# Attention of a streaming-encoder layer: 128-query pieces, paired banks, fewer copies at a block's end

## The chip, the cores and the metric

The kernel runs on one core of a Trainium2 chip. Its time is device microseconds (us) of one execution. The kernel before takes 4123.1 us, the median of three runs (4122.56 to 4125.78). A profiled execution, from which all durations below come, took 4126.18 us, with a span of 4124.6 us between its first and last instruction.

The engines are PE (TensorE, matmuls), DVE (VectorE, elementwise work), ACT (ScalarE, activations and copies), POOL (GpSimd) and SP (SyncE, which issues DMA transfers). PE writes its results to PSUM, a memory of eight banks, each of which holds 512 fp32 numbers per partition; ACT and DVE read them from there.

## The reference, cut to what matters

One layer of a trunk: a joint input projection, a recurrent group (RG-LRU), a group of eight attention heads, an output projection, a mixture of experts and a per-layer embedding, over 4096 tokens of width 1024. The change touches the attention alone. Its reference, for blocks of 128 queries and 8 heads of width 64:

```python
for qb in range(S // Q_BLOCK):
    lo, hi = qb * Q_BLOCK, (qb + 1) * Q_BLOCK
    s = jnp.einsum('bhqd,bhkd->bhqk', q[:, :, lo:hi], k[:, :, :hi]) * scale
    s = s + cum_logf[:, :, lo:hi, None] - cum_logf[:, :, None, :hi]
    mask = jnp.arange(hi)[None, :] <= jnp.arange(lo, hi)[:, None]
    pr = jax.nn.softmax(jnp.where(mask, s, -jnp.inf), axis=-1)
    outs.append(jnp.einsum('bhqk,bhkd->bhqd', pr, v[:, :, :hi]))
```

`cum_logf` is a running sum of the logarithms of forget gates, so a key's weight falls with its distance from the query.

## The kernel before, in words

The program runs in stages: projection and recurrence (to about 1060 us of the profiled execution), attention (to about 1790 us), output projection and router, then the experts and the embedding. Attention works in 64 units: a unit is a head `h` and a block `b` of 512 queries. Scores are laid out with 128 keys on the partitions and queries along the row, so one matmul takes a tile of 128 keys and up to 512 queries.

For each head, ranked by how fast its gates forget, two tables set what is computed. `NEAR` is the reach of the keys that enter the softmax, `WIN` the reach of those that are only looked at. For each unit `pieces` (L542) makes two lists of banks: `near` and `far`. A bank is a list of pieces (key tile, first query, last query, place in the bank). In the kernel before a piece is 256, 384 or 512 queries wide; a piece that reaches fewer queries is widened to 256, and two of 256 share a bank. The four key tiles on the diagonal are pieces of 512, 384, 256 and 256 queries; the triangle is masked by a small bf16 matmul (`mask`, L606).

Each unit passes four steps:

- The max pass (`max_pass`, L649): one matmul for each piece into a bank of the pool `psM` (tile `psm`), then a running maximum `mx` over the banks: ACT copies the first bank (L667), DVE folds in one piece after the other (L669). POOL reduces `mx` over the partitions (L672) and writes the result into the row of queries `Q2` and `Q3`, by which later matmuls subtract it.
- The scores (`scores`, L690): near banks are taken two at a time, as a group. For each piece two matmuls (L703, L704) fill a bank `pss` of the pool `psS`, and ACT takes two exponentials of each bank, one rounded for the matmul (`ph`, L708) and one full (`pf`, L709).
- The correction (`low`, L714): DVE computes `pl`, which is `pf` less `ph`, in one instruction over both banks where they are equally long (L720), and otherwise in one for each (L723).
- The values (`pv`, L725): for each piece one fp32 matmul of `ph` (L743) and four narrow bf16 matmuls (L751 to L753), two groups after the group's scores. They accumulate in `O`, two banks that neighbouring units use in turn: `acc` is the unit's own, `alt` the other one's row 96, where a part of value row 0 is kept. At a block's end ACT makes three copies out of `O` (L763 to L765), DVE one sum (L766), and POOL issues two DMA transfers (L768, L769).

The far banks are only looked at (`look`, L678): one matmul for each piece into a bank `psf` of the pool `psM`, and one exponential with a running sum (L688), whose result decides whether a head's far keys can be left out.

The pools `psM` and `psS` have three banks each, `O` has two: all eight. The order of PE's instructions is written out by the loop at the end of the stage: scores of the group's first bank, a step of the max pass (and a look) from `between`, the second bank, another step, remaining looks, and the values of the group two before. The max pass runs 14 banks ahead (`LEAD`). The other engines' order is set by a scheduler.

Of the kernel before, what the change touches and what calls it, by code (L numbers as in the profile page):

```python
# [10 lines left out]
F32 = mybir.dt.float32  # L11
# [32 lines left out]
NFB = 8  # L44
# [15 lines left out]
def hybrid_block(ctx: ExitStack, tc: tile.TileContext, I, out, T, caps, dbg=None, upto=9):  # L60
# [456 lines left out]
    with tc.tile_pool(name="dk0", bufs=1) as dk0, tc.tile_pool(name="dq", bufs=1) as dqp, \  # L517
            tc.tile_pool(name="dp", bufs=2) as dp, tc.tile_pool(name="dk1", bufs=1) as dk1, \
            tc.tile_pool(name="dob", bufs=2) as dob, \
            tc.tile_pool(name="psM", bufs=3, space=PSUM) as psM, tc.tile_pool(name="psS", bufs=3, space=PSUM) as psS, \  # L520
# [11 lines left out]
        maskb = dqp.tile([P, 2 * P], BF16, name="maskb")  # L532
        V.tensor_copy(identb, ident)
        V.memset(maskb, 0.0)
        V.memset(maskb[:, 0:P], NEG)
        G.affine_select(maskb[:, P:2 * P], maskb[:, P:2 * P], pattern=[[1, P]], compare_op=ALU.is_ge, fill=NEG,
# [4 lines left out]

        def pieces(u):  # L542


            r, b = units[u]
            nn, nw = NEAR[r] // P, WIN[r] // P
            near = [[(4 * b, 0, 512, 0)], [(4 * b + 1, P, 512, 0)]]
            half = [(4 * b + 2, 256, 512), (4 * b + 3, 256, 512)]
            rest = []
            for j in range(1, min(4 * b, nw) + 1):  # L550
                kt = 4 * b - j
                w = 0 if j > nn else max(256, min(512, (nn - j + 1) * P))
                f = min(512, (nw - j + 1) * P)
                if w > 256:
                    near.append([(kt, 0, w, 0)])
                elif w:
                    half.append((kt, 0, w))
                if f > w:
                    rest.append((kt, w, min(512, max(f, w + 256))))
            near += [[(*p, 256 * i) for i, p in enumerate(half[k:k + 2])] for k in range(0, len(half), 2)]  # L560
            far = []
            for kt, c0, c1 in sorted(rest, key=lambda p: p[1] - p[2]):
                for bank in far:
                    at = bank[-1][3] + bank[-1][2] - bank[-1][1]
                    if at + c1 - c0 <= 512:
                        bank.append((kt, c0, c1, at))
                        break
                else:
                    far.append([(kt, c0, c1, 0)])
            return near, far  # L570
# [35 lines left out]
        def mask(ps, b, kt, c0, at):  # L606
            d = kt - 4 * b
            if d == 3:
                PE.matmul(ps[:, at:at + 256], identb, maskb, start=False, stop=True)
            elif d >= 0:  # L610
                o = at + d * P - c0
                PE.matmul(ps[:, o:o + P], identb, maskb[:, P:2 * P], start=False, stop=True)  # L612
# [65 lines left out]
        def look(u, k):  # L678
# [3 lines left out]
            bank = plan[u][1][k]  # L682
            ps = psM.tile([P, 512], F32, tag="m", name="psf")
            for kt, c0, c1, at in bank:
                PE.matmul(ps[:, at:at + c1 - c0], K2[i][0:KR, kt * P:(kt + 1) * P], Q3[qi][0:KR, c0:c1], start=True, stop=True)
            n = length(bank)
            jf = dp.tile([P, 512], BF16, tag="jf", bufs=2, name="jf")
            S.activation(jf[:, 0:n], ps[:, 0:n], AF.Exp, bias=fbias, accum_out=gm[:, u, k:k + 1])  # L688

        def scores(u, banks, between):  # L690
# [5 lines left out]
            pf = dp.tile([P, 2, 512], F32, tag="pf", bufs=2, name="pf")  # L696
            for a, bank in enumerate(banks):
                ps = psS.tile([P, 512], F32, tag="s", name="pss")
                for kt, c0, c1, at in bank:
# [3 lines left out]
                    PE.matmul(ps[:, at:e], K1[i][:, ks], q1[:, c0:c1], start=True, stop=False)  # L703
                    PE.matmul(ps[:, at:e], K2[i][0:KR, ks], Q2[qi][0:KR, c0:c1], start=False, stop=not dg)  # L704
                    if dg:
                        mask(ps, b, kt, c0, at)
                n = length(bank)
# [1191 lines left out]
```

## Time and profile before

| | us |
|---|---|
| median of three runs | 4123.1 |
| profiled execution | 4126.18 |
| its span | 4124.6 |
| attention, 1080 to 1780 us: length | 700.0 |
| of it ACT busy | 634.0 |
| of it PE busy | 629.4 |
| of it DVE busy | 519.8 |
| of it POOL busy | 334.9 |

An instruction's duration runs from its start until its result is written; the next one may start before that. The distance from one start to the next is called a step below. PE's durations are modelled and overlap one another, so its busy time is not a measure of how much work it could take.

### The profile page before, as it was taken

The numbers are of one execution on the slowest core, as the hardware profiler recorded it, in microseconds if no ns is written. First come the engines' busy times: TensorE is split into PE (matmuls) and PEld (weight loads), VectorE is DVE, ScalarE is ACT, GpSimd is POOL, SyncE is SP. The second block draws the span as 40 slices with busy tenths as digits, with TensorE's granted clock in tenths as the row PEclk, the third lists the DMA queues.
The fourth block names the chain that finished last, engine by engine and source line by source line (L and its number), as shares of the span: only waits on it lengthen the run. The fifth ranks groups of instructions, "written<-read, shape, count | busy, mean of one in ns | idle before, by whom it ended". The sixth has DMA issues, their size and how long they took to land. (4 is left out here: it accounts for less than half of the span.)

```text
span 4124.6 us, 63126 instructions
## 1 busy us (share of the span) xinstructions
PE 3908.7 (95%) x21955; PEld 3191.5 (77%) x21955; DVE 2662.6 (65%) x5513; ACT 2240.8 (54%) x3823; POOL 598.1 (15%) x719
## 2 busy tenths in 40 slices
PE   8999998999788889979999699999999999999999
PEld 7878876777455556657788488899998999988887
DVE  5445456777777777778887345566665566566666
ACT  4333235777688999953333335556565555552222
POOL 0000000000343445601111111101111111100000
PEclk9999998999899999989999899999999999999999
DMA  6445343221443445554443546666776666664454
GB/s 221 132 128 162 124 133 103 67 67 49 113 122 104 118 120 137 146 149 133 138 122 98 187 142 201 209 229 234 239 234 208 215 228 227 224 233 159 158 181 146
DMA packets 331451, 653.59 MB, mean 158 GB/s; under 512 B 40170, under 2 KB 163306, under 8 KB 331123
## 3 DMA queue, kind: packets, MB, share of 16 engines
q1 hardware_dynamic: 263729, 516.96, 40.0%
q0 software_dynamic: 30880, 81.75, 6.0%
q10 hardware_dynamic: 36514, 50.74, 3.9%
q8 instruction: 177, 2.90, 0.3%
q14 instruction: 151, 1.24, 0.1%
HBM read 507.24 MB, written 147.31 MB: 159 GB/s over the span
## 5 line engine op out<-in xcount | busy, mean ns | idle before, releaser
L105 DVE TENSOR_TENSOR ul<-raw,uh 128x1024 fp32r<-128x1024 f32 x410 | 497.1, 1222 | 155.2 <-ACT uh L104 154.7
L111 PE MATMUL psg<-xh,uh 128*128 128x256 f32 (+5 forms) x1600 | 510.9, 319 | 0.8 <-ACT xh L107 0.8
L112 PE MATMUL psg<-xl,uh 128*128 128x256 f32 (+5 forms) x1600 | 504.9, 316 | 0.0
L113 PE MATMUL psg<-xh,ul 128*128 128x256 f32 (+5 forms) x1600 | 504.7, 315 | 0.0
L104 ACT CAST uh<-raw 128x1024 fp32r<-128x1024 f32 x410 | 424.0, 1046 | 58.6 <-DMA raw<-in_w_exp_dram 58.2
L111 PEld LDWEIGHTS psg<-xh,uh 128*128 128x128 f32 x1600 | 303.7, 190 | 13.8 <-ACT xh L107 1.2
L112 PEld LDWEIGHTS psg<-xl,uh 128*128 128x128 f32 x1600 | 303.9, 190 | 9.4 <-DVE xl L108 0.5
L113 PEld LDWEIGHTS psg<-xh,ul 128*128 128x128 f32 x1600 | 303.7, 190 | 8.7
L669 DVE TENSOR_TENSOR mx<-psm,mx 128x256 f32<-128x256 f32 (+2 forms) x438 | 220.1, 510 | 95.2 <-PE psm L662 56.3
L708 ACT ACTIVATE ph<-pss 128x512 fp32r<-128x512 f32 (+1 forms) x386 | 224.3, 581 | 57.7 <-PE pss L612 20.8
L111 PE MATMUL psy<-uh,hid 128*128 128x512 f32 (+2 forms) x608 | 250.2, 412 | 0.0
L113 PE MATMUL psy<-uh,hid 128*128 128x512 f32 (+2 forms) x608 | 240.1, 395 | 0.0
L112 PE MATMUL psy<-ul,hid 128*128 128x512 f32 (+2 forms) x608 | 240.1, 395 | 0.0
L170 PE MATMUL z<-wh,xh 128*128 128x512 f32 x768 | 227.3, 400 | 8.7 <-ACT wh L107 8.7
L170 PE MATMUL z<-wl,xh 128*128 128x512 f32 x768 | 224.4, 397 | 2.0 <-DVE wl L108 2.0
L709 ACT ACTIVATE pf<-pss 128x512 f32<-128x512 f32 (+1 forms) x386 | 225.4, 584 | 0.0
L170 PE MATMUL z<-wh,xl 128*128 128x512 f32 x768 | 222.4, 395 | 0.0
L111 PE MATMUL pso<-wo,yh 128*128 128x512 f32 x512 | 206.8, 404 | 5.9 <-ACT yh L104 5.9
L112 PE MATMUL z<-xl,wh 128*128 128x512 f32 x512 | 202.1, 396 | 9.3 <-DVE xl L105 9.3
L224 ACT ACTIVATE sq<-z,rcol 128x512 f32<-128x512 f32 x64 | 43.6, 686 | 306.3 <-PE z L170 306.2
L112 PE MATMUL pso<-wo,yh 128*128 128x512 f32 x512 | 204.5, 399 | 5.3 <-issue 5.3
L111 PE MATMUL pg<-uh,xh 128*128 128x512 f32 x512 | 205.8, 402 | 1.2 <-ACT xh L104 1.2
(468 smaller groups left out, 10197.3 us busy)
## 6 DMA issues: line engine op xcount, KB each, us to landing
raw<-in_w_exp_dram SPq DMA_DIRECT2D x408, 512.0 KB
xraw<-in_xT_dram ACTq DMA_DIRECT2D x128, 256.0 KB
raw<-d_y SPq DMA_DIRECT2D x64, 512.0 KB
d_v<-vt SPq DMA_DIRECT2D x32, 520.0 KB
VT<-d_v SPq DMA_DIRECT2D x64, 260.0 KB
d_x<-x SPq DMA_DIRECT2D x16, 1028.0 KB
xr<-in_x_dram SPq DMA_DIRECT2D x32, 512.0 KB
K<-d_kh SPq DMA_DIRECT2D x128, 128.0 KB
```

The lines of the kernel that those rows point to most:

```text
L104: S.copy(hi, src)
L105: V.tensor_sub(lo, src, fv(hi))
L111: PE.matmul(ps, sh, mh, start=first, stop=False)
L112: PE.matmul(ps, sh, ml, start=False, stop=False)
L113: PE.matmul(ps, sl, mh, start=False, stop=last)
L170: PE.matmul(zs[j], x[k // 2][:, xs], w[k % 2][:, j * 512:(j + 1) * 512], start=(kc == 0 and k == 0), stop=(kc == KC - 1 and k == 2))
L224: S.activation(sq[:, j, :], zs[j], AF.Square, scale=r)
L669: V.tensor_tensor(mx[:, c0:c1], ps[:, at:at + c1 - c0], mx[:, c0:c1], op=ALU.max)
L708: S.activation(ph[:, a, 0:n], ps[:, 0:n], AF.Exp)
L709: S.activation(pf[:, a, 0:n], ps[:, 0:n], AF.Exp)
```

## The change

Pieces become exactly as wide as their reach, in multiples of 128 queries, and `packed` puts them into banks, longest first, as many as fit; full banks come first. The diagonal's fourth piece is 128 wide and its mask, like the others, 128 columns. Counted by the two versions of `pieces` over the 64 units: the near lists have 502 pieces as before; 116 of the 234 that were 256 queries wide are now 128; their columns go from 182,656 to 167,808, their banks from 386 to 339 (318 full ones), their groups from 205 to 191 (137 of two full banks, 33 of one full bank, 21 others). The far lists have 329 pieces, 93,824 columns and 190 banks before and after.

The pool `psS` now has two buffers of two banks, and `psM` two banks. A group's scores fill one buffer of `psS`, and then one exponential `ph` and one `pf` go over both banks. `look` takes two far banks at once, fills a buffer of `psS` instead of one of `psM`, and takes one exponential over both: 108 in place of 190. Looks no longer stand in `between`, but all behind the group's scores. `low` always works bank by bank. At a block's end ACT keeps one copy; DVE copies row 96 of the other bank to a row `rw` (one buffer) and adds to it; POOL issues three DMA transfers in place of two.

```diff
-NFB = 8
+NFB = 4
...
-            tc.tile_pool(name="psM", bufs=3, space=PSUM) as psM, tc.tile_pool(name="psS", bufs=3, space=PSUM) as psS, \
+            tc.tile_pool(name="psM", bufs=2, space=PSUM) as psM, tc.tile_pool(name="psS", bufs=2, space=PSUM) as psS, \
...
+        def packed(pieces):
+
+            banks = []
+            for kt, c0, c1 in sorted(pieces, key=lambda p: p[1] - p[2]):
+                for bank in banks:
+                    if length(bank) + c1 - c0 <= 512:
+                        bank.append((kt, c0, c1, length(bank)))
+                        break
+                else:
+                    banks.append([(kt, c0, c1, 0)])
+            return sorted(banks, key=lambda b: -length(b))
...
-            near = [[(4 * b, 0, 512, 0)], [(4 * b + 1, P, 512, 0)]]
-            half = [(4 * b + 2, 256, 512), (4 * b + 3, 256, 512)]
-            rest = []
+            near = [(4 * b + d, d * P, 512) for d in range(4)]
+            far = []
             for j in range(1, min(4 * b, nw) + 1):
-                kt = 4 * b - j
-                w = 0 if j > nn else max(256, min(512, (nn - j + 1) * P))
+                w = max(0, min(512, (nn - j + 1) * P))
                 f = min(512, (nw - j + 1) * P)
...
+                if w:
+                    near.append((4 * b - j, 0, w))
                 if f > w:
-                    rest.append((kt, w, min(512, max(f, w + 256))))
...
+                    far.append((4 * b - j, w, f))
+            return packed(near), packed(far)
...
-            if d == 3:
-                PE.matmul(ps[:, at:at + 256], identb, maskb, start=False, stop=True)
-            elif d >= 0:
+            if d >= 0:
                 o = at + d * P - c0
-                PE.matmul(ps[:, o:o + P], identb, maskb[:, P:2 * P], start=False, stop=True)
+                PE.matmul(ps[:, o:o + P], identb, maskb, start=False, stop=True)
...
-            bank = plan[u][1][k]
-            ps = psM.tile([P, 512], F32, tag="m", name="psf")
-            for kt, c0, c1, at in bank:
-                PE.matmul(ps[:, at:at + c1 - c0], K2[i][0:KR, kt * P:(kt + 1) * P], Q3[qi][0:KR, c0:c1], start=True, stop=True)
-            n = length(bank)
-            jf = dp.tile([P, 512], BF16, tag="jf", bufs=2, name="jf")
-            S.activation(jf[:, 0:n], ps[:, 0:n], AF.Exp, bias=fbias, accum_out=gm[:, u, k:k + 1])
+            ps = psS.tile([P, 2, 512], F32, tag="s", name="psf")
+            banks = plan[u][1][2 * k:2 * k + 2]
+            for a, bank in enumerate(banks):
+                for kt, c0, c1, at in bank:
+                    PE.matmul(ps[:, a, at:at + c1 - c0], K2[i][0:KR, kt * P:(kt + 1) * P], Q3[qi][0:KR, c0:c1], start=True, stop=True)
+            jf = dp.tile([P, 1024], BF16, tag="jf", bufs=1, name="jf")
+
+            n = 512 * (len(banks) - 1) + length(banks[-1])
+            assert len(banks) == 1 or length(banks[0]) == 512
+            S.activation(jf[:, 0:n], ps.rearrange("p a n -> p (a n)")[:, 0:n], AF.Exp, bias=fbias, accum_out=gm[:, u, k:k + 1])
...
+            ps = psS.tile([P, 2, 512], F32, tag="s", name="pss")
             for a, bank in enumerate(banks):
-                ps = psS.tile([P, 512], F32, tag="s", name="pss")
...
-                n = length(bank)
-                S.activation(ph[:, a, 0:n], ps[:, 0:n], AF.Exp)
-                S.activation(pf[:, a, 0:n], ps[:, 0:n], AF.Exp)
                 if a == 0:
                     between()
+            n = 512 * (len(banks) - 1) + length(banks[-1])
+            assert len(banks) == 1 or length(banks[0]) == 512
+            for t in (ph, pf):
+                S.activation(t.rearrange("p a n -> p (a n)")[:, 0:n], ps.rearrange("p a n -> p (a n)")[:, 0:n], AF.Exp)
             return u, banks, ph, pl, pf
...
-            ns = [length(bank) for bank in banks]
-            if len(ns) == 2 and ns[0] == ns[1]:
-                if a == 0:
-                    n = ns[0]
-                    V.tensor_tensor(pl[:, :, 0:n], pf[:, :, 0:n], fv(ph)[:, :, 0:n], op=ALU.subtract)
-            elif a < len(ns):
-                n = ns[a]
+            if a < len(banks):
+                n = length(banks[a])
                 V.tensor_tensor(pl[:, a, 0:n], pf[:, a, 0:n], fv(ph)[:, a, 0:n], op=ALU.subtract)
...
+                rw = dob.tile([1, 512], F32, tag="rw", bufs=1, name="rw")
                 sm = dob.tile([64, 512], F32, tag="sm", name="sm")
-                ob = dob.tile([65, 512], F32, tag="ob", name="ob")
+                ob = dob.tile([64, 512], F32, tag="ob", name="ob")
+
                 S.copy(sm, acc[64:128])
-                S.copy(sm[0:1], alt[96:97])
-                S.copy(ob[64:65], acc[64:65])
-                V.tensor_tensor(ob[0:64], acc[0:64], sm, op=ALU.add)
+                V.tensor_copy(rw, alt[96:97])
+                V.tensor_tensor(ob, acc[0:64], sm, op=ALU.add)
+                V.tensor_tensor(rw, acc[0:1], rw, op=ALU.add)
                 et = ACE if u == len(units) - 1 else PLE_
-                E.dma_start(d_o[bass.ds(head(h, 2, et), HD), bs], ob[0:64])
-                E.dma_start(d_den[bass.ds(head(h, 0, et), 1), bs], ob[64:65])
+                E.dma_start(d_o[bass.ds(head(h, 2, et), 1), bs], rw)
+                E.dma_start(d_o[bass.ds(head(h, 2, et) + 1, HD - 1), bs], ob[1:HD])
+                E.dma_start(d_den[bass.ds(head(h, 0, et), 1), bs], sm[0:1])
...
-                mine = list(range(len(far)))
+                nf = (len(far) + 1) // 2
+                mine = list(range(nf))
                 if ng > 1:
-                    mine = mine[len(far) * max(0, g - 1) // (ng - 1):len(far) * g // (ng - 1)]
+                    mine = mine[nf * max(0, g - 1) // (ng - 1):nf * g // (ng - 1)]
...
-                    if mine:
-                        look(u, mine.pop(0))
                     if prev:
```

How this moves instructions on ACT, around the end of a block of the third head. The two buffers of `O` carry numbers, the other tiles are named as above; sizes are partitions by columns. Before:

```order
L688 ACTIVATE jf,gm<-psf,fbias 128x512
L708 ACTIVATE ph<-pss 128x512
L709 ACTIVATE pf<-pss 128x512
L763 COPY sm<-O_8693 64x512
L765 COPY ob<-O_8693 1x512
L764 COPY sm<-O_8694 1x512
L708 ACTIVATE ph<-pss 128x384
L709 ACTIVATE pf<-pss 128x384
```

And after, around the end of a block of the same head:

```order
L709 ACTIVATE ph<-pss 128x1024
L709 ACTIVATE pf<-pss 128x1024
L685 ACTIVATE jf,gm<-psf,fbias 128x1024
L758 COPY sm<-O_8692 64x512
L709 ACTIVATE ph<-pss 128x1024
L709 ACTIVATE pf<-pss 128x1024
```

Two of the three copies are gone from ACT, and each exponential covers both banks of a group.

On DVE, the instructions around a block's end before:

```order
L669 TENSOR_TENSOR mx<-psm,mx 128x512
L720 TENSOR_TENSOR pl<-pf,ph 128x1024
L669 TENSOR_TENSOR mx<-psm,mx 128x512
L766 TENSOR_TENSOR ob<-O_8693,sm 64x512
L723 TENSOR_TENSOR pl<-pf,ph 128x384
```

And after:

```order
L663 TENSOR_TENSOR mx<-psm,mx 128x384
L663 TENSOR_TENSOR mx<-psm,mx 128x128
L759 COPY rw<-O_8693 1x512
L716 TENSOR_TENSOR pl<-pf,ph 128x512 x2
L760 TENSOR_TENSOR ob<-O_8692,sm 64x512
L761 TENSOR_TENSOR rw<-O_8692,rw 1x512
L663 TENSOR_TENSOR mx<-psm,mx 128x384
```

Two instructions on one row of `O` have come to DVE at each block's end, with corrections and maxima of other groups queued between and behind them.

On PE, one group with a look after the change, from its scores to the values of the group two before:

```order
L700 MATMUL pss<-q_13895,K_8677 128x384
L701 MATMUL pss<-Q_8698,K_8679 128x384
L700 MATMUL pss<-q_13895,K_8677 128x128
L701 MATMUL pss<-Q_8698,K_8679 128x128
L656 MATMUL psm<-Q_8700,K_8679 128x384
L656 MATMUL psm<-Q_8700,K_8679 128x128
L700 MATMUL pss<-q_13895,K_8677 128x256
L701 MATMUL pss<-Q_8698,K_8679 128x256
...
L680 MATMUL psf<-Q_8704,K_8679 128x256 x2
L680 MATMUL psf<-Q_8704,K_8679 128x384
L736 MATMUL O_8692<-ph,VT_8681 128x512 x2
```

The step of the max pass stands between the two banks of a pair that now get their exponentials together, and the look fills the other buffer of the same pool.

## Rows read from the trace of the kernel before

**Rows 1.** Busy time by stretch: us, PE, PEld, DVE, ACT, POOL, PE clock, DMA share, GB/s.

```profile
1080.00:1780.00 700.00, 629.43 (x4808) 406.94 (x4806) 519.78 (x879) 634.02 (x1408) 334.88 (x434) 0.98 0.46 123
1558.00:1708.00 150.00, 144.17 (x1167) 94.91 (x1163) 119.64 (x195) 144.35 (x322) 84.53 (x107) 1.00 0.53 143
```

**Rows 2.** Waits from 1058 to 1782 us: us in total, times, longest.

```profile
PE O L743 <- ACT sm L764: 30.5, 33, 2.6
PE psf L685 <- ACT mx L667: 17.8, 11, 1.9
```

**Rows 3.** ACT's groups, 1080 to 1780 us: count, busy us, mean ns, idle before.

```profile
L688 ACT ACTIVATE jf<-psf,fbias 128x512 bf16<-128x512 f32 x179 | 127.1, 714 | 0.1
L764 ACT COPY sm<-O 1x512 f32<-1x512 f32 x62 | 35.9, 580 | 1.5
L765 ACT COPY ob<-O 1x512 f32<-1x512 f32 x62 | 35.8, 577 | 1.5
```

**Rows 4.** Timeline, ACT and PE, at a block's end: start, us, instruction.

```profile
1501.58 0.58 ACT L765 COPY ob<-O 1x512 f32<-1x512 f32 x1
1502.18 0.58 ACT L764 COPY sm<-O 1x512 f32<-1x512 f32 x1
1502.78 0.49 ACT L708 ACTIVATE ph<-pss 128x384 fp32r<-128x384 f32 x1
1502.81 0.67 PE L743 MATMUL O<-ph,VT 128*128 128x512 f32 x2 [1.36 <-ACT sm L764]
```

**Rows 5.** Timeline, ACT: steps of exponentials of 512 and 384 columns.

```profile
1505.16 0.62 ACT L708 ACTIVATE ph<-pss 128x512 fp32r<-128x512 f32 x1
1505.63 0.64 ACT L709 ACTIVATE pf<-pss 128x512 f32<-128x512 f32 x1
1506.11 0.74 ACT L688 ACTIVATE jf<-psf,fbias 128x512 bf16<-128x512 f32 x1
...
1506.77 0.53 ACT L688 ACTIVATE jf<-psf,fbias 128x256 bf16<-128x256 f32 x1
...
1508.76 0.50 ACT L708 ACTIVATE ph<-pss 128x384 fp32r<-128x384 f32 x1
1509.13 0.51 ACT L709 ACTIVATE pf<-pss 128x384 f32<-128x384 f32 x1
```

**Rows 6.** DVE's groups, 1080 to 1780 us.

```profile
L723 DVE TENSOR_TENSOR pl<-pf,ph 128x512 bf16<-128x512 f32 x135 | 100.0, 742 | 19.3 <-ACT pf L709 17.3
L720 DVE TENSOR_TENSOR pl<-pf,ph 128x1024 bf16<-128x1024 f32 x68 | 97.1, 1428 | 37.4 <-ACT pf L709 36.9
L669 DVE TENSOR_TENSOR mx<-psm,mx 128x256 f32<-128x256 f32 x232 | 94.5, 420 | 32.7 <-PE psm L609 15.3 <-PE psm L662 13.3 <-DVE mx L669 0.5
L723 DVE TENSOR_TENSOR pl<-pf,ph 128x384 bf16<-128x384 f32 x113 | 75.6, 669 | 13.3 <-ACT pf L709 10.9
L669 DVE TENSOR_TENSOR mx<-psm,mx 128x512 f32<-128x512 f32 x90 | 61.9, 688 | 31.2 <-PE psm L662 29.6
...
L766 DVE TENSOR_TENSOR ob<-O,sm 64x512 f32<-64x512 f32 x62 | 42.1, 679 | 13.1 <-ACT sm L764 12.2
```

**Rows 7.** A DVE copy of 512 columns out of PSUM, whole trace.

```profile
L1536 DVE COPY ys<-psy 128x512 f32<-128x512 f32 x70 | 48.0, 685 | 60.0 <-PE psy L113 60.0
```

**Rows 8.** Timeline, PE: steps within a group, and two block starts of the sixth head.

```profile
1510.55 0.39 PE L703 MATMUL pss<-q,K 128*128 128x512 f32 x1
1510.78 0.40 PE L704 MATMUL pss<-Q,K 128*128 128x512 f32 x1
...
1584.87 0.50 PE L703 MATMUL pss<-q,K 128*128 128x512 f32 x1
...
1594.34 0.50 PE L703 MATMUL pss<-q,K 128*128 128x512 f32 x1
```

**Rows 9.** POOL's transfers, 1080 to 1780 us; then one's KB and us to landing.

```profile
L768 POOL DMA_DIRECT2D d_o<-ob x62 | 34.3, 553 | 109.7 <-DVE ob L766 96.1 <-DVE mn L834 7.1 <-DVE pl L720 4.7
...
d_den<-ob POOLq DMA_DIRECT2D x62, 2.0 KB, 2.6
```

More of the change, by code (lines that the diff above doesn't have):

```diff
@@ L531, in hybrid_block @@
         identb = dqp.tile([P, P], BF16, name="identb")
-        maskb = dqp.tile([P, 2 * P], BF16, name="maskb")
+        maskb = dqp.tile([P, P], BF16, name="maskb")
         V.tensor_copy(identb, ident)
         V.memset(maskb, 0.0)
-        V.memset(maskb[:, 0:P], NEG)
-        G.affine_select(maskb[:, P:2 * P], maskb[:, P:2 * P], pattern=[[1, P]], compare_op=ALU.is_ge, fill=NEG,
+        G.affine_select(maskb, maskb, pattern=[[1, P]], compare_op=ALU.is_ge, fill=NEG,
                         base=0, channel_multiplier=-1)
@@ L546, in pieces @@
             nn, nw = NEAR[r] // P, WIN[r] // P
-            near = [[(4 * b, 0, 512, 0)], [(4 * b + 1, P, 512, 0)]]
-            half = [(4 * b + 2, 256, 512), (4 * b + 3, 256, 512)]
-            rest = []
+            near = [(4 * b + d, d * P, 512) for d in range(4)]
+            far = []
             for j in range(1, min(4 * b, nw) + 1):
-                kt = 4 * b - j
-                w = 0 if j > nn else max(256, min(512, (nn - j + 1) * P))
+                w = max(0, min(512, (nn - j + 1) * P))
                 f = min(512, (nw - j + 1) * P)
[L554 to L557, printed above, removed]
+                if w:
+                    near.append((4 * b - j, 0, w))
                 if f > w:
-                    rest.append((kt, w, min(512, max(f, w + 256))))
[L560 to L570, printed above, removed]
+                    far.append((4 * b - j, w, f))
+            return packed(near), packed(far)
         def length(bank):
@@ L702, in scores @@
                     e = at + c1 - c0
-                    PE.matmul(ps[:, at:e], K1[i][:, ks], q1[:, c0:c1], start=True, stop=False)
-                    PE.matmul(ps[:, at:e], K2[i][0:KR, ks], Q2[qi][0:KR, c0:c1], start=False, stop=not dg)
+                    PE.matmul(ps[:, a, at:e], K1[i][:, ks], q1[:, c0:c1], start=True, stop=False)
+                    PE.matmul(ps[:, a, at:e], K2[i][0:KR, ks], Q2[qi][0:KR, c0:c1], start=False, stop=not dg)
                     if dg:
-                        mask(ps, b, kt, c0, at)
-                n = length(bank)
-                S.activation(ph[:, a, 0:n], ps[:, 0:n], AF.Exp)
-                S.activation(pf[:, a, 0:n], ps[:, 0:n], AF.Exp)
+                        mask(ps[:, a], b, kt, c0, at)
                 if a == 0:
                     between()
+            n = 512 * (len(banks) - 1) + length(banks[-1])
+            assert len(banks) == 1 or length(banks[0]) == 512
+            for t in (ph, pf):
+                S.activation(t.rearrange("p a n -> p (a n)")[:, 0:n], ps.rearrange("p a n -> p (a n)")[:, 0:n], AF.Exp)
             return u, banks, ph, pl, pf
```

## The prediction

> **What bounds the kernel now.** First the busy time of each engine by stretch, since the change touches one stage alone. In the attention's 700 us ACT is busy for 634 and PE for 629 [rows 1]; the reader should see two engines at nine tenths, DVE at 520 and POOL at 335. Next the waits, to tell which of the two holds the other. PE's largest wait is for the last of ACT's copies at a block's end, 30.5 us in 33 cases, and the next is a look's matmul that waits, 17.8 us, because ACT has not yet copied the first bank of a max pass [rows 2]. The timeline of one such end shows it: two one-row copies start 0.60 us apart, and PE's first value matmul of the next block stands still for 1.36 us until the second is done [rows 4]. So ACT's queue is the limit and PE runs on its credit. How close an engine comes to the whole of a stretch it limits is 634 / 700 = 0.906 for the stage, and 144.35 / 150 = 0.962 in the sixth and seventh heads [rows 1].
>
> PE's 629 us is no measure of its work: two matmuls of 512 columns start 0.23 us apart but are shown 0.39 and 0.40 us long [rows 8]. The Trainium skill (Perfetto Trace Analysis, "Identifying the Most-Contended Engine") says that matmul busy time does not tell how close TensorE is to its limit; the trace agrees here, since steps are little more than half of durations.
>
> **The change part by part.**
>
> *ACT.* Two of three copies go at each of 63 block ends: 0.58 us long each [rows 3] but 0.60 from start to start [rows 4], so 63 x 1.20 = 76 us. Each exponential has a fixed part and a part by columns: 0.475 us at 512 columns and 0.37 at 384 [rows 5] give 0.82 ns for a column and 0.055 us fixed. Exponentials go from 2 x 386 to 2 x 191, so 390 x 0.055 = 21 us, and 2 x 14,848 columns fewer x 0.82 ns = 24 us. No row shows one over two banks; if crossing the border cost a fixed part again the 21 us would be nothing, and if each of the 382 paid a bank's 0.055 us twice more it would be a loss of 21, so this term lies between -21 and 21; I take 21, because the steps at 384 and 512 columns lie on one line, and ACT is not the limit afterwards at either end. A look is 0.71 us long at 512 columns [rows 3], and the next one starts 0.66 us after it [rows 5], of which 0.42 is columns, so 82 fewer looks save 82 x 0.24 = 20 us. ACT's work falls by about 141 us, to some 493.
>
> *PE.* The near columns pass PE five times in all (one maximum, two scores, one value matmul, one pass of narrow ones side by side): 14,848 x 5 / 512 x 0.23 us [rows 8] = 33 us less. Whether a piece of 128 columns costs half of one of 256 no row here shows; if a piece cost the same at any width nothing would be saved, so the term lies between 0 and 33; I take 33, since the two steps of 0.23 us [rows 8] hold no stretch in which nothing streams that I can see. What PE needs when it does not wait: a block of the sixth head takes 1594.34 - 1584.87 = 9.47 us [rows 8]; its 5 x 2,816 + 1,536 columns are 30.5 x 0.23 = 7.0 us, so some 2.4 us a block go on mode changes, masks and short waits. After the change: (5 x 167,808 + 93,824) / 512 x 0.23 + 64 x 2.4 = 419 + 154 = 573 us. The waits in [rows 2] lose their cause: the one-row copies are no longer on ACT, and looks no longer take a bank of the max pass.
>
> *DVE.* At each block's end it gets a copy of one row, which at 512 columns out of PSUM takes 0.685 us [rows 7], and a sum like the present one, 0.679 us [rows 6]: 63 x 1.364 = 86 us more. The price lies between 63 x 0.48 (ACT's fastest step of 512) x 2 = 60 and, should each hold the queue for a further 0.6 us because its input is late, 160. The corrections were 273 us in three groups [rows 6] and two small ones; they become 318 at 0.742 and 21 shorter ones, 245 us: 28 less. Of the maxima 116 become 128 columns wide; (688 - 420) / 256 = 1.05 ns for a column [rows 6] makes 0.134 us each, 15 us less. In sum 86 - 28 - 15 = 43 more, 563 us. The one row `rw` has a single buffer, so a block's copy must wait until the transfer of the one before has landed, 2.6 us after its issue [rows 9]; blocks follow one another by more than 5 us, POOL's queue lies between, and I cost it at nothing; in the eight shortest blocks it could be 1 us each. Queued behind that copy on DVE stand the corrections of the group that PE needs next.
>
> *POOL.* One more transfer at 0.553 us [rows 9] is 62 x 0.553 = 34 us, which takes it to 369 us: off the path. DVE does pay a little: 135 corrections from SBUF alone average 742 ns where maxima of the same width out of PSUM take 688 [rows 6]. The Trainium skill (GPSIMD Engine Reference, "1. Specifications") says that GpSimd shares its SBUF interfaces with VectorE and contends with instructions that read two SBUF inputs; the two means agree. By that rule the surplus of 54 ns on 318 corrections, 17 us, would grow with POOL's busy share, by about 4 us; the sum does not use this.
>
> *The buffers.* A group's two exponentials now start only when both banks are full, and PE may refill the buffer only when both are done. Where the next pair falls on the same buffer, and it does wherever a look stands between, the loop is: fill, 4 x 0.23 = 0.92 us, with a step of the max pass of about 0.25 in it; some 0.3 until ACT starts (an estimate: the 0.17 us by which a matmul's duration exceeds its step [rows 8], and as much again for the signal); two exponentials of 0.055 + 1024 x 0.82 ns = 0.895 each; 0.12 until the last is written: 3.4 us. The mean group today takes 700 / 205 = 3.41 us, and the new one at PE's own work 573 / 191 = 3.0. So the loop costs up to 0.4 us in the 108 groups with a look, 43 us if nothing overlaps it, and nothing in the others; a look's own exponential, 0.24 + 0.84 = 1.08 us, fits into the fill.
>
> **The sum.** After the change PE needs 573 us, DVE 563, ACT 493. The limit passes from ACT to PE and DVE together. At the share that the limit reaches now, 573 / 0.906 = 632 us; with the loop instead, 573 + 43 = 616, and some for DVE. I take 630: 70 us less than 700. The profiled execution had 4126.2 us, 3.1 above the median of the runs, so 4126.2 - 70 = 4056, or 4053 by the median. The stages around it have no instruction changed and keep their time. If DVE's new work comes at its upper bound (+74 us, 637 / 0.906 = 703) the gain is gone; at shares of 0.962 and of 0.86, about as far below as that is above, the stage takes 596 or 666 us, which gives 4019 to 4089 as the likeliest case's own range.
>
> **The rivals.**
>
> *PE alone sets the pace, at the share of the sixth and seventh heads.* For it: there PE waits almost nowhere now. Against it: DVE stands at the same level and is coupled to it by two banks. 573 / 0.962 = 596, 104 us less: 4019, and to 4005 where DVE's row work hides.
>
> *DVE becomes the limit and gives most of it back.* For it: 86 us more work on an in-order queue, where the correction that PE needs next stands behind a copy that waits for PE, and the max pass has two banks in place of three. Against it: DVE had 180 us to spare. At a share of 0.83, 563 / 0.83 = 678: 22 less, 4101.
>
> *PE's busy time is its work.* Then only the columns count: 33 us less, 4090. Against it stand the steps [rows 8]; this is inside the range and I give it no chance of its own beside the last.
>
> *The pair loop makes it slower.* The step of the max pass stands between the two banks of a fill. If DVE holds its bank back by 0.7 us each time, the loop becomes 4.1 us in the 108 groups with a look, and with 3.4 in the other 83 the stage is 443 + 282 = 725: 25 more, 4148. It decides from a mean of 700 / 191 = 3.66 us a group, that is from about 0.3 us of such delay in every group. Against it: today the maxima wait for PE, not the other way round, in the groups of [rows 6].
>
> *Nothing comes of it*, because each saving meets a delay of its own size, 4123.
>
> **How the numbers follow.** Forecast 0.58, PE alone 0.15, DVE as the limit 0.15, slower 0.07, nothing 0.05. A measurement of this kernel can tell a change of about 0.2%, 8 us. Faster by more than that: 0.58 + 0.15 + 0.15 = 0.88; the same 0.05; slower 0.07. The range runs from 4008 to 4105, which takes in PE alone down to its share and DVE as the limit, and leaves out the last two cases and the tails.
>
> **What would show it.** ACT's two one-row copies gone and its busy time in the stage near 500 us; no wait of PE's value matmuls for ACT, at most one for the row copy on DVE; DVE's share of the stage above 0.85 (it is 0.74 now), with row copy and row sum at 0.6 to 0.7 us each; a stage of about 630 us between the same neighbours. Wrong would be: PE waiting for ACT at the start of score pairs for over 60 us in all (the loop), for DVE at the max pass for over 60 us (DVE as the limit), row copies that wait for a transfer, or exponentials of 1024 columns whose step is well over 0.9 us.

## The result, and the profile after

The changed kernel takes 4087.23 us (median of four runs, 4084.99 to 4090.58) against 4124.44 (four runs, 4122.56 to 4126.82): a ratio of 0.9911, with an interval from 0.9899 to 0.9924. That is 37 us faster, where 70 were forecast. Its profiled execution has a span of 4089.0 us.

The length of the attention is taken below from one operation that every kernel here has 64 times, DVE's sum at a block's end. This view gives its count, its shortest, median and longest duration in ns, and when the first and the last one start. It is read from one execution of each kernel, which lay up to 6 us off the median of that kernel's runs, so differences of a few us in it say nothing.

```profile
L760 DVE TENSOR_TENSOR ob<-O,sm x64: 670/682/685, 1095.5 to 1752.4; 64x512 f32<-64x512 f32 x64
```

From first to last that is 656.9 us; before the change the same sum runs from 1098.9 to 1788.0, 689.1 us. So 32 of the 35.6 us by which the spans of the two profiled executions differ come from the attention. They are not spread evenly: by the starts of each head's last sum the first five heads became 1.8 to 12.6 us shorter, and the last three 6.0, 4.1 and 4.1 us longer. By the same edges [rows 1] took 700 us; the busy times of the shorter stretch now, in the columns of [rows 1]:

```profile
1080.00:1742.00 662.00, 604.21 (x4762) 401.02 (x4762) 533.30 (x1016) 495.77 (x726) 371.85 (x493) 0.98 0.47 130
```

ACT has lost 138 us and is busy for three quarters of the stretch; DVE has gained 14. PE's granted clock is 0.98 in both stretches, so it has little part in the difference. The waits that answer to [rows 2], from 1058 to 1750 us (us in total, times, longest):

```profile
PE O L746 <- DVE rw L761: 26.5, 38, 3.4
PE psm L656 <- DVE mx L663: 13.5, 10, 6.6
PE pss L700 <- ACT pf L709: 12.8, 32, 0.9
...
DVE rw L759 <- DMA d_o<-rw: 9.7, 5, 3.2
...
PE O L736 <- DVE rw L759: 5.8, 6, 2.2
...
POOL d_o L764 <- DMA d_o<-rw: 78.3, 36, 3.8
```

PE's wait for ACT's last copy, 30.5 us, is gone, and 26.5 + 5.8 = 32.3 us for DVE's work on the row stand in its place. Below, POOL waits 78.3 us: its transfer of the block goes out only after that of the row, issued just before it to the same tensor, has landed.

The groups of ACT, 1080 to 1742 us, that answer to [rows 3] and [rows 5], and those of DVE that answer to [rows 6]:

```profile
L709 ACT ACTIVATE ph<-pss 128x1024 fp32r<-128x1024 f32 x136 | 139.7, 1027 | 112.8 <-PE pss L701 87.0 <-PE pss L606 23.9
L709 ACT ACTIVATE pf<-pss 128x1024 f32<-128x1024 f32 x135 | 137.9, 1021 | 0.0
L685 ACT ACTIVATE jf<-psf,fbias 128x1024 bf16<-128x1024 f32 x68 | 76.5, 1125 | 0.0
L758 ACT COPY sm<-O 64x512 f32<-64x512 f32 x62 | 36.1, 583 | 6.3 <-PE O L736 4.7
```

```profile
L716 DVE TENSOR_TENSOR pl<-pf,ph 128x512 bf16<-128x512 f32 x315 | 226.3, 741 | 77.7 <-ACT pf L709 67.7 <-PE pss L606 6.8 <-PE psm L656 2.6
L759 DVE COPY rw<-O 1x512 f32<-1x512 f32 x62 | 42.9, 693 | 17.9 <-DMA d_o<-rw 9.7 <-PE O L746 6.2 <-PE psm L656 0.6
L760 DVE TENSOR_TENSOR ob<-O,sm 64x512 f32<-64x512 f32 x62 | 42.1, 678 | 3.6 <-ACT sm L758 2.2
L761 DVE TENSOR_TENSOR rw<-O,rw 1x512 f32<-1x512 f32 x61 | 40.8, 669 | 0.0
L663 DVE TENSOR_TENSOR mx<-psm,mx 128x128 f32<-128x128 f32 x115 | 32.7, 285 | 2.4
```

ACT now waits for PE's scores, 113 us ahead of `ph`: it is no limit any more. But DVE, with 129 us to spare, is no steady limit either: it waits 67.7 us for exponentials. What it does to PE shows at one block's end in the sixth head: DVE, then PE's one long wait there (in brackets).

```profile
1596.89 0.69 DVE L759 COPY rw<-O 1x512 f32<-1x512 f32 x1
1597.51 1.27 DVE L716 TENSOR_TENSOR pl<-pf,ph 128x512 bf16<-128x512 f32 x2
1598.82 0.68 DVE L760 TENSOR_TENSOR ob<-O,sm 64x512 f32<-64x512 f32 x1
1599.42 0.67 DVE L761 TENSOR_TENSOR rw<-O,rw 1x512 f32<-1x512 f32 x1
...
1604.77 0.69 DVE L716 TENSOR_TENSOR pl<-pf,ph 128x512 bf16<-128x512 f32 x1 [2.75 <-ACT pf L709]
```

```profile
1600.15 0.39 PE L746 MATMUL O<-ph,VT 128*1 128x512 bf16 x1 [1.22 <-DVE rw L761]
```

From the row copy to the end of the row sum is a chain of 3.2 us with two corrections inside; over all 64 blocks it takes 3.5 us on average. PE's narrow matmul of the next block writes row 96 of the bank that the last of them still reads, and starts 0.06 us after it. From 1602.0, two microseconds after the chain's end, DVE stands idle for 2.75 us: it has the time, but not there.

### The profile page after: what moved, and what is told of

The parts are those of the page before. It is cut to its first block, busy times and chain, and to the rows that moved or that the text cites. A ratio compares the mean times of both kernels' runs of the same rounds, so it can differ in the third digit from the quotient of the medians.

```text
span 4089.0 us, 62859 instructions
## 1 busy us (share of the span) xinstructions
PE 3888.6 (95%) x21955; PEld 3189.4 (78%) x21955; DVE 2680.6 (66%) x5661; ACT 2102.9 (51%) x3141; POOL 635.7 (16%) x782
## 5 line engine op out<-in xcount | busy, mean ns | idle before, releaser
L104 ACT CAST uh<-raw 128x1024 fp32r<-128x1024 f32 x410 | 424.0, 1046 | 58.7 <-DMA raw<-in_w_exp_dram 57.9
L716 DVE TENSOR_TENSOR pl<-pf,ph 128x512 bf16<-128x512 f32 (+3 forms) x339 | 237.0, 722 | 77.7 <-ACT pf L709 67.7
L709 ACT ACTIVATE ph<-pss 128x1024 fp32r<-128x1024 f32 (+3 forms) x191 | 173.1, 906 | 140.5 <-PE pss L701 107.0
L663 DVE TENSOR_TENSOR mx<-psm,mx 128x256 f32<-128x256 f32 (+3 forms) x438 | 198.9, 469 | 26.9 <-PE psm L656 16.1
L111 PE MATMUL pso<-wo,yh 128*128 128x512 f32 x512 | 206.6, 404 | 8.4 <-ACT yh L104 5.8
L1532 POOL DMA_INDIRECT d_y<-ys,ids x74 | 92.6, 1251 | 745.4 <-ACT xh L107 341.3
L700 PE MATMUL pss<-q,K 128*128 128x512 f32 (+3 forms) x502 | 193.8, 386 | 13.0 <-ACT pf L709 12.8
```

The costliest lines, as they stand in the source:

```text
L104: S.copy(hi, src)
L111: PE.matmul(ps, sh, mh, start=first, stop=False)
L663: V.tensor_tensor(mx[:, c0:c1], ps[:, at:at + c1 - c0], mx[:, c0:c1], op=ALU.max)
L700: PE.matmul(ps[:, a, at:e], K1[i][:, ks], q1[:, c0:c1], start=True, stop=False)
L709: S.activation(t.rearrange("p a n -> p (a n)")[:, 0:n], ps.rearrange("p a n -> p (a n)")[:, 0:n], AF.Exp)
L716: V.tensor_tensor(pl[:, a, 0:n], pf[:, a, 0:n], fv(ph)[:, a, 0:n], op=ALU.subtract)
```

## The experiments

Four theories went into them. A: the chain of row work on DVE at a block's end holds PE, as ACT's copies did before. B: the row's own transfer holds POOL, and through it the short blocks of the last head. C: the score pairs, and the looks between them, wait for their two buffers. D: a piece of 128 queries costs PE nearly what one of 256 did, so the columns saved are not time saved. All ratios are to the kernel before.

### The block's end

**The row sum before the block's sum.**

```diff
 V.tensor_copy(rw, alt[96:97])
+V.tensor_tensor(rw, acc[0:1], rw, op=ALU.add)
 V.tensor_tensor(ob, acc[0:64], sm, op=ALU.add)
-V.tensor_tensor(rw, acc[0:1], rw, op=ALU.add)
```

> The changed kernel with the row sum on DVE put ahead of the block's sum (rw before ob). Theory A (the block-end chain: the next block's narrow matmuls wait for the row sum on DVE, which stands behind the block's sum, which waits for ACT's copy): that wait, 26.5 us in the changed kernel, moves to the block's sum, which ends about 0.6 us earlier after the copy; 10 to 25 us less than the changed kernel's 4087, so 4062 to 4077. Theory B (POOL, which waits for the row's transfer to land before it issues the block's): within 4 us of 4087, and POOL's wait stays near 78 us. Theory C (the loop of score pairs through two buffers): no change.

4094.59 us, 0.9926 [0.9912, 0.9939]; attention 661.9 us. That is 7 us more, where theory A expected 10 to 25 less, though the intervals overlap. PE now waits for whichever comes last:

```profile
PE O L746 <- DVE ob L761: 24.4, 34, 2.9
```

The order inside the chain is not what costs. Its length, 3.5 us on average here too, stayed the same.

**One transfer for the block.**

```diff
-V.tensor_tensor(rw, acc[0:1], rw, op=ALU.add)
+V.tensor_tensor(ob[0:1], acc[0:1], rw, op=ALU.add)
...
-E.dma_start(d_o[bass.ds(head(h, 2, et), 1), bs], rw)
-E.dma_start(d_o[bass.ds(head(h, 2, et) + 1, HD - 1), bs], ob[1:HD])
+E.dma_start(d_o[bass.ds(head(h, 2, et), HD), bs], ob)
```

> The changed kernel with the row sum written over row 0 of the block's sum, so that one transfer of 64 rows leaves in place of one row and 63. Theory B: POOL's 78 us of waiting for the row's transfer go, DVE's row copies no longer wait for a landing (9.7 us), and the last head, where POOL has no idle time but that wait, gets 8 to 15 us shorter: 4067 to 4079, with the gain in the last head alone. Theory A: the wait of the narrow matmuls for the row sum stays near 26 us, and 4083 to 4090. Theory C: no change.

4100.22 us, 0.9941 [0.9928, 0.9955]; attention 665.9 us. The time is longer than any theory expected, but between the last block-end sums of the seventh and the last head lie 56.0 us in place of 64.6, as theory B expected. In the changed kernel POOL shows it (start, us, instruction, wait ahead of it):

```profile
1699.62 0.50 POOL L763 DMA_DIRECT2D d_o<-rw  x1
1703.54 0.54 POOL L764 DMA_DIRECT2D d_o<-ob  x1 [3.42 <-DMA d_o<-rw]
1704.19 0.49 POOL L765 DMA_DIRECT2D d_den<-sm  x1
1704.76 1.78 POOL L666 PARTITION_ALL_REDUCE mr<-mx  x1
```

The reduction of the next maxima stands behind it. The Trainium skill (DMA: Bandwidth & Descriptors, "Anatomy of one DMA — SWDGE (gpsimd) path") says that a small transfer costs about 2 us whatever its size, most of it until the write is confirmed; the trace agrees, since the 36 waits of POOL for 2 KB average 2.2 us, the longest 3.8. In six of the other seven heads the kernel lost 1.6 to 5.2 us. PE waits 34.9 us for the last sum there, in place of 26.5, and the chain on DVE takes 3.9 us on average in place of 3.5, with three instructions of other groups inside where there were two. Why the new sum lets more of them in is not shown.

**Looks behind the value matmuls**, alone, and with the row sum first.

```diff
-for k in mine:
-    look(u, k)
 prev.append(cur)
 if len(prev) > 2:
     pv(prev.pop(0))
+for k in mine:
+    look(u, k)
```

> The changed kernel with each look put behind the values of the group two before instead of ahead of them, so that ACT's copy at a block's end stands ahead of the look's exponential. Theory A: the copy runs about 1 us earlier, and the wait of the narrow matmuls for the row sum falls from 26.5 us to under 8; 15 to 30 us less, 4057 to 4072. Theory B: no change beyond 4 us. Theory C: the look's exponential now ends later, at the time at which the next pair's first is due, so 5 to 20 us more, 4092 to 4107.

> The changed kernel with looks behind the values and also the row sum ahead of the block's sum on DVE: with the copy early on ACT, the block's sum is the only thing behind it. Theory A: the wait for DVE at the first narrow matmuls of a block, 16.5 us with late looks alone, falls below 8, and the time to 4072 to 4082. If DVE's queue as a whole is what that wait shows, and not the order within a block's end: 4083 to 4092, as with either change alone.

4087.18 us, 0.991 [0.9896, 0.9924], and 4087.47, 0.9916 [0.9902, 0.9929]: both as the changed kernel. The waits at a block's start fall from 32.3 to 20.5 and 19.5 us, and those of the max pass for DVE rise from 13.5 to 20.5 and 21.0; the attention takes 652.2 and 654.2 us. Theory A expected 5 to 30 us less; theory B for the one, and the rival named for the other, no change. Moving PE's work about one chain lets it wait elsewhere.

**No row work at all.**

```diff
-V.tensor_copy(rw, alt[96:97])
 V.tensor_tensor(ob, acc[0:64], sm, op=ALU.add)
-V.tensor_tensor(rw, acc[0:1], rw, op=ALU.add)
...
-E.dma_start(d_o[bass.ds(head(h, 2, et), 1), bs], rw)
-E.dma_start(d_o[bass.ds(head(h, 2, et) + 1, HD - 1), bs], ob[1:HD])
+E.dma_start(d_o[bass.ds(head(h, 2, et), HD), bs], ob)
```

> The changed kernel without the work on value row 0 at a block's end: no copy of row 96, no row sum, one transfer of 64 rows (row 0 of each head then lacks its part and holds a wrong sum). DVE has 86 us less and POOL one transfer and its wait less. If the chain of copy and sums on DVE is what holds PE at a block's start, PE's wait of 32 us for the row falls under 12, the last head goes from 64.6 to about 55 us, and the time to 4050 to 4060. If PE's own work and the pair buffers set the pace, the waits turn up elsewhere (scores for the exponential, max pass), and only the last head's 8 us come: 4075 to 4080.

4166.38 us, 1.0109 [1.0093, 1.0124], which no theory expected. The loss lies outside the attention: what it hands on differs, and the experts' stage, whose work follows the routing, casts 434 blocks of weights in place of 410 (L104). Its attention is the shortest of all:

```profile
L758 DVE TENSOR_TENSOR ob<-O,sm x64: 670/674/684, 1095.4 to 1712.2; 64x512 f32<-64x512 f32 x64
```

Of its waits this one is left at a block's start:

```profile
PE O L746 <- DVE ob L758: 6.1, 9, 2.2
```

616.8 us, 40.1 less than the changed kernel, with 6.1 us in place of 32.3. The last head takes 48.8 us in place of 64.6. So the row work, at 84 us of DVE's time and one more transfer, costs 40 us of the stage in these two executions. That of the changed kernel lies 3.4 us above the median of its runs, and this one 5.9 below, so 30 to 40 us is what can be said.

**The accumulator freed after one DVE operation.**

```diff
+S.copy(rw, alt[96:97])
 S.copy(sm, acc[64:128])
-V.tensor_copy(rw, alt[96:97])
 V.tensor_tensor(ob, acc[0:64], sm, op=ALU.add)
-V.tensor_tensor(rw, acc[0:1], rw, op=ALU.add)
+V.tensor_tensor(rw, rw, sm[0:1], op=ALU.subtract)
+V.tensor_tensor(ob[0:1], ob[0:1], rw, op=ALU.add)
...
-E.dma_start(d_o[bass.ds(head(h, 2, et), 1), bs], rw)
-E.dma_start(d_o[bass.ds(head(h, 2, et) + 1, HD - 1), bs], ob[1:HD])
+E.dma_start(d_o[bass.ds(head(h, 2, et), HD), bs], ob)
```

> The changed kernel with another block end: ACT copies row 96 to rw and then the 64 rows to sm; DVE makes one sum out of PSUM (ob = acc + sm), and corrects row 0 with two operations in SBUF alone (rw = rw - sm row 0, ob row 0 += rw); one transfer of 64 rows. DVE has as many operations as the changed kernel, but PSUM is free after one of them. If PE is held by the chain out of PSUM, its waits for DVE at a block's start fall from 32 us to under 15, the last head goes to about 56 us, and the time to 4060 to 4070. If ACT's copies hold PE instead, as before the change, a wait for ACT's sm or rw of 15 us or more takes the place, and the time is 4075 to 4090.

4080.29 us, 0.9899 [0.9884, 0.9914]. Its block-end sum, and its waits:

```profile
L760 DVE TENSOR_TENSOR ob<-O,sm x64: 670/683/684, 1096.7 to 1739.5; 64x512 f32<-64x512 f32 x64
```

```profile
PE pss L700 <- ACT pf L709: 26.2, 53, 1.4
PE psm L656 <- DVE mx L663: 12.0, 9, 6.6
...
PE O L746 <- DVE ob L760: 9.0, 23, 2.1
...
PE O L736 <- ACT rw L758: 1.8, 2, 1.5
```

The attention is 14.1 us shorter, and the time 7 us, not the 17 to 27 that theory A gave it (some 4 us of the gap between the two lies in how far the two profiled executions were from their medians). The waits at a block's start fall from 32.3 to 10.8 us, but those of score matmuls for the exponentials double; ACT has one more copy in its queue, which would do it, though no run shows that by itself. It is the fastest kernel that was run and 43 us below the one before; its interval overlaps that of the changed kernel, so that it beats this one too is likely rather than settled.

### The parts of the change

**Pieces of 128 queries and packing alone**, in the kernel before (`pieces`, `packed`, `mask` and its tile from the change); **the new block end alone**; **both, without pairs**; **pieces and pairs with the old block end**; and **pairs and the new block end with the old widths**, of which this is the main part of the diff against the changed kernel:

```diff
-near = [(4 * b + d, d * P, 512) for d in range(4)]
+near = [(4 * b + d, min(d, 2) * P, 512) for d in range(4)]
...
-w = max(0, min(512, (nn - j + 1) * P))
+w = 0 if j > nn else max(256, min(512, (nn - j + 1) * P))
...
-far.append((4 * b - j, w, f))
+far.append((4 * b - j, w, min(512, max(f, w + 256))))
```

> The kernel before with the new pieces and their packing alone; pools of three banks, exponentials and looks of one bank, looks between the banks and the block's end as before. Theory D (a narrow piece costs PE nearly what a wide one did, since the mode changes around masks and narrow matmuls stay): PE's steps of score matmuls keep their sum, about 150 us in the stage, and what is gained is ACT's, 94 exponentials fewer: 10 to 20 us less than before, 4104 to 4114. The prediction's own term (33 us of columns on PE, and ACT's relief): 30 to 45 us less, 4079 to 4094.

> The kernel before with the new end of a block alone (one copy on ACT, two row instructions on DVE, three transfers on POOL). If ACT's queue was the limit, as predicted, 76 us of copies less give 25 to 50 us, 4074 to 4099, with the wait of the value matmuls for ACT's copies gone. Theory A (the wait only changes its engine): the next block now waits for the row sum on DVE, and it gains 0 to 20 us, 4104 to 4124; the last head gets longer through POOL's wait for the row's transfer.

> The kernel before with 128-query pieces and the new block end, but without pairs: three single buffers for the scores, three for maxima and looks, one exponential for each bank, one look for each far bank. Against the changed kernel ACT has 41 us more work (fixed parts of exponentials and looks), some 536 of a stage of 660, and DVE the same. If pairing counts only through ACT's work, it is worth nothing once the block end is off ACT: 4085 to 4095, equal to the changed kernel. If the pairs carry a part of the gain of their own (groups that start with both banks free, more looks out of the way of the maxima), the two other parts alone add up to what they gave alone, 22 and 6 us: 4095 to 4103.

> The changed kernel with the block's end of before (three copies on ACT, one sum on DVE, two transfers). If the new end is what gave the gain: 20 to 40 us more than 4087, 4107 to 4127. If the wait only changed its engine (theory A): within 10 us of 4087, the last head about 8 us shorter as POOL waits for no row, the heads with much work on ACT longer.

> The changed kernel with the piece widths of before: no piece under 256 queries, the diagonal's fourth piece 256 wide with a mask of 256, packed longest first as in the change; 182,656 near columns and 386 near banks again in 205 groups (125 of two full banks), looks as many columns as before; everything else as changed (pairs, looks, block end). If a matmul's price goes by its columns (the term of the prediction), PE gets 33 us more and DVE some 40 (15 in maxima, 25 in corrections): 4120 us or over, and PE's busy share stays. If a narrow piece costs PE nearly what a piece of twice its width did, PE's work without waits rises by under 20 us from its 591 and the time by 10 to 20, to about 4100.

| pieces | pairs | block end | us | ratio [interval] | attention |
|---|---|---|---|---|---|
| new | old | old | 4101.39 | 0.9951 [0.9937, 0.9964] | 672.9 |
| old | old | new | 4118.0 | 0.9988 [0.9979, 0.9997] | 685.7 |
| new | old | new | 4116.01 | 0.9986 [0.9977, 0.9995] | 678.5 |
| new | new | old | 4116.54 | 0.9989 [0.998, 0.9999] | 684.5 |
| old | new | new | 4117.71 | 0.9986 [0.9977, 0.9995] | 683.8 |
| new | new | new | 4087.23 | 0.9911 [0.9899, 0.9924] | 656.9 |

Narrow pieces give some 20 us by themselves and 30 in the paired kernel (4117.71 less 4087.23). The row with old pieces and all else new also brings back 47 banks and 14 groups, and takes the exponentials of 35 groups bank by bank. Both times lie between what theory D and what the prediction's term would give, and the steps in the changed kernel say why (start, us):

```profile
1491.81 0.23 PE L606 MATMUL pss<-maskb,identb 128*128 128x128 bf16 x1
1491.84 0.31 PE L700 MATMUL pss<-q,K 128*128 128x128 f32 x1
1491.99 0.27 PE L701 MATMUL pss<-Q,K 128*128 128x128 f32 x1
1492.10 0.23 PE L606 MATMUL pss<-maskb,identb 128*128 128x128 bf16 x1
...
1494.47 0.34 PE L700 MATMUL pss<-q,K 128*128 128x384 f32 x1
1494.65 0.34 PE L701 MATMUL pss<-Q,K 128*128 128x384 f32 x1
1494.83 0.22 PE L700 MATMUL pss<-q,K 128*128 128x128 f32 x1
1494.89 0.27 PE L701 MATMUL pss<-Q,K 128*128 128x128 f32 x1
1495.00 0.46 PE L656 MATMUL psm<-Q,K 128*128 128x384 f32 x2
...
1495.46 0.28 PE L701 MATMUL pss<-Q,K 128*128 128x256 f32 x1
1495.58 0.23 PE L606 MATMUL pss<-maskb,identb 128*128 128x128 bf16 x1
1495.62 0.37 PE L700 MATMUL pss<-q,K 128*128 128x256 f32 x1
1495.83 0.28 PE L701 MATMUL pss<-Q,K 128*128 128x256 f32 x1
```

A first score matmul of 384 columns takes 0.18 us to the next start, one of 128 takes 0.06: a third, though it is shown 0.22 us long. Behind a mask, as on the diagonal, one of 128 takes 0.15 and one of 256 takes 0.21, so the columns count there too. But the second score matmul of a narrow piece takes 0.11 us until a mask or a matmul of the max pass starts, and one of 256 columns takes 0.12: there nothing is saved. By the count of PE's work that is used further below, all score matmuls together take 192 us before, 187 with narrow pieces alone and 191 in the changed kernel, where the columns would save 13. So theory D holds in good part for the scores, and what PE saves lies in the other passes.

Pairs or the new block end, put on narrow pieces one without the other, each take back 15 us, and together they give 14. On the old pieces the new block end alone, which takes two of three copies off ACT, gave 5 us (4118.0 against 4122.74), as theory A expected: the wait only changed its engine.

```profile
PE O L753 <- DVE rw L768: 29.3, 28, 3.8
```

For the pairs the waits of the kernel with the old block end point to the cause:

```profile
PE O L736 <- ACT sm L757: 40.7, 56, 1.3
PE pss L700 <- ACT pf L709: 27.9, 56, 1.1
```

With narrow pieces alone the first of these was 21.1 us, and the second did not occur. Three copies of 0.58 us stand in ACT's queue among exponentials that are now 1.02 us long, and both the accumulator and the score buffer come free later. So in the paired kernel, unlike the one before, the new end is worth 29 us. In the kernel without pairs the waits of the looks for ACT stand out:

```profile
PE psf L679 <- ACT jf L682: 33.6, 32, 1.9
PE O L747 <- DVE rw L762: 14.6, 17, 2.4
...
PE psm L656 <- ACT jf L682: 10.6, 11, 1.8
```

There a look holds a bank of the max pass until ACT gets to it: 33.6 + 10.6 us, where the kernel with narrow pieces alone has 9.1 + 3.1. But that kernel's looks wait for DVE's maxima instead:

```profile
PE psf L679 <- DVE mx L663: 29.0, 41, 1.7
```

Over all causes PE's looks wait 44.2 us there and 41.9 without pairs, so they do not explain the 15 us. Why the kernel without pairs is that much slower, where 4085 to 4103 was expected, is not settled.

**Looks one bank at a time, in the max pass's two banks**, everything else as changed (`look` and its count as before the change).

```diff
-ps = psS.tile([P, 2, 512], F32, tag="s", name="psf")
-banks = plan[u][1][2 * k:2 * k + 2]
+bank = plan[u][1][k]
+ps = psM.tile([P, 512], F32, tag="m", name="psf")
```

> The changed kernel with looks one far bank at a time again, in the two banks of the max pass, 190 exponentials in place of 108, so that score pairs have both buffers to themselves. Theory C: PE's wait of score matmuls for the exponentials (12.8 us) goes and ACT's idle time before score pairs shrinks; 5 to 15 us less, 4072 to 4082. Theories A and B: the looks now wait for banks of the max pass and ACT does 20 us more; 5 to 25 us more, 4092 to 4112, with the wait of the narrow matmuls for the row sum unchanged or larger.

4264.82 us, 1.0346 [1.0332, 1.036]; attention 831.1 us. No theory expected a loss of this size.

```profile
PE psf L679 <- DVE mx L663: 98.1, 124, 2.4
```

With two banks for maxima and looks, looks stand behind DVE's maxima in 124 cases. These waits are 98 of the 174 us; and over the stage PE's granted clock is 0.89 of full speed on average (the column after POOL's), where the changed kernel has 0.98: for 22% of the stage it stood at 1.2 GHz, the lower of its two levels, in place of 2.4. So a part of the loss is slower matmuls:

```profile
1094.00:1925.00 831.00, 679.64 (x4777) 434.91 (x4775) 532.51 (x1000) 526.53 (x892) 374.17 (x495) 0.89 0.37 101
```

The wait of 12.8 us of score matmuls for exponentials is gone, as theory C expected, but a stage so much slower would do that by itself. That the looks passed to the pairs' pool is what makes two banks for the max pass bearable.

## Why the prediction was right, and where its size was off

Right was the direction. That ACT's queue was the limit, with PE running on its credit, is not borne out: with two of its three copies off ACT alone the kernel gained 5 us, and narrow pieces, which relieve PE, ACT and DVE, gained 21.

*ACT.* Forecast 493 us, measured 495.8. The exponential over two banks has a step of 0.90 to 0.92 us (0.895 forecast), so crossing the border costs at most 0.025 us, and the term of 21 us was taken at the right end.

```profile
1591.59 1.03 ACT L709 ACTIVATE ph<-pss 128x1024 fp32r<-128x1024 f32 x1
1592.51 1.03 ACT L709 ACTIVATE pf<-pss 128x1024 f32<-128x1024 f32 x1
```

*PE.* The term of 33 us by columns holds in part. In size I can bound it only: when all that a step has above its columns (at 512 in 0.228 us) and 0.13 us is counted as waiting, PE's work in the stage is 610 us before, 591 after and 611 with the old widths, and 584 with narrow pieces alone, so 20 to 26 us rather than 33. The second score matmuls, 116 of them at 0.06 us that were not saved, are 7 us of what is missing. Without the row work the same count gives 577, near the forecast of 573: the rest seems to be small delays at the block ends, which that count cannot tell from work.

*DVE.* Copy and sum of the row at 0.693 and 0.669 us are as priced: 84 us for 62 blocks, against 86 for 63. Busy time rose by 14 us and not 43; maxima and corrections fell by 22 and 37 rather than 15 and 28, and the stretch is 38 us shorter. Its share is 0.81, under the 0.85 named as a sign.

*What failed* is the step "The waits in [rows 2] lose their cause: the one-row copies are no longer on ACT". The wait for the look's bank did go. That at a block's start did not: it is 32.3 us where it was 30.5. Its cause was not the copies' place on ACT alone, but that a reader of the accumulator stands at the end of a chain in a busy queue. Before, PE waited for the third of three copies on ACT, 1.8 us on average from the first one's start to the last one's end; now it waits for the third of three operations on DVE, which take 3.5 us with what stands between them. The prediction named what is queued on DVE, and then charged the row work as load under a share of 0.906. With it fails "I cost it at nothing", of the single row and its transfer: DVE waited 9.7 us for it, which the prediction had listed as a sign of being wrong, and POOL's queue held up the last head. All of the row work together is the 30 to 40 us that leaving it out takes off the stage. How that divides is shown in part only: with as many operations on DVE, but the accumulator free after one of them and one transfer, the stage gets back 14 us, so the length of the chain and the transfer are a part of it, and what DVE's load has of the rest is open. Without the row work the stage is 72 us shorter than before. The sum had said 70, but with that work on DVE in it, so the agreement is chance.

*The rivals.* "PE alone sets the pace" took its share of 0.962 from the sixth and seventh heads; just these became 6.0 and 4.1 us longer. The pair loop, forecast at up to 43 us, shows 12.8 us of waits. Of "DVE becomes the limit and gives most of it back" the place was right and the mechanism wrong: 4101 was priced from its total, but it is idle for a fifth of the stretch. "PE's busy time is its work" would have given 4090, close to the measured time, and by chance: PE's busy time fell by 25 us, the stage by 32, and with the row work out of the way the stage falls by a further 40 at much the same number of columns.

*Contention.* The surplus that the prediction left out of its sum did not grow: POOL's busy share rose from 0.48 to 0.56, and a correction takes 741 ns where it took 742 [rows 6]. The Trainium skill (GPSIMD Engine Reference, "1. Specifications") has GpSimd and VectorE contend for SBUF; this step of POOL's share shows nothing of it.

## What to carry to other kernels

When work moves from a full engine to one with time to spare, ask what waits for its last instruction, and count the chain from the first input to that release, with what the new queue puts in between: a share of busy time doesn't tell it. Free the buffer that the next block needs with as few instructions as possible, and do the rest from SBUF. The parts of such a change can't be added up: put on the first, two of the three here lost 15 us each alone and gained 14 together.

## What was not expected of the hardware

A matmul of 128 columns is shown 0.22 to 0.27 us long, but takes 0.06 us before another of its chain, 0.15 behind a mask, and 0.11 as the last of a chain before a mask or a matmul of the max pass, no less than one of 256. One exponential over two PSUM banks had a step of 0.90 to 0.92 us, where one over a single bank has 0.47 to 0.49. And 2 KB to a tensor that the next transfer on the same queue also writes held that queue for 78.3 us in 36 blocks, 2.2 us each.
